# Moving half of a convolution's multiplier out of the attention loop and into a seven-product step

## The chip, the cores and the metric

The kernel runs on one core of one Trainium2 chip. The metric is device time in microseconds (us). Before the change it is 686.75 us, the median of 3 runs (686.73 to 687.19).

## The reference, cut to what matters

One layer on x with 512 positions and 1024 channels. After a norm, one projection `h @ w_in` gives the multiplier B, C and the input of a gated convolution (512 channels each), q, k and v of 8 heads, and the gates. Cut:

```python
cb, cc, cin, q, k, v, f_logit, g_logit = jnp.split(proj, split_idx, axis=-1)
u = causal_dwconv(cc * cin, conv_mix_w[l])
y_conv = (cb * u) @ w_out_conv[l]
...
o = forgetting_attention(q, k, v, log_f)
y_attn = o @ w_out_attn[l]
x = x + (g_conv * y_conv + g_attn * y_attn) @ w_o[l]
```

The multiplier of the convolution, `cb`, is what the change computes in another way. A feed-forward part and a last norm follow.

## The kernel before

**Numbers.** All products are in fp32r. Each fp32 operand is kept as a high and a low part, and a product is three matmuls (high by high, low by high, high by low). A weight block arrives by DMA as a tile `raw`; ScalarE (ACT) makes the high part `wh` (L275), VectorE (DVE) the low part `wl` (L282), in two buffers each, so that block n+2 can be split only when TensorE (PE) is done with block n. A matmul of these steps has 256 columns.

**Plain and seven-product steps.** A plain output block of 128 channels by 512 positions takes 8 input blocks, 3 matmuls, 2 halves: 48 matmuls (`proj`). `seven` computes a pair of output blocks over pairs of input blocks and halves of the positions with 7 products where 8 would do (a Strassen-Winograd form): 84 matmuls for the pair and not 96. It needs sums of input blocks (`xt`, split into `xtq` by `x_split`), and sums of weights: a chunk `P` holds three weight blocks as they are for each step, a chunk `F` four sums of weight blocks, which DMAs add up in DRAM ahead (`make_forms`: a copy on SP's queue, then an accumulating DMA on POOL's queue, three times over, six transfers for a form). A pair is two steps, so four chunks: P, F, P, F, with 18, 24, 18 and 24 matmuls. Its results come out of four PSUM banks by DVE and ACT work (`z1`, `m1`, `u3`, `m2`, then one `fin` for each block).

**Order of the work.** Projections for v, q0, k0, q1, k1 come first. Then the attention loop: 37 rounds, one for each unit (pair of heads, head, block of 128 queries) and five more to finish. A round has the scores of one unit (`s`), a part of the remaining projections as filling (`p_in`; a list `late` of 16 blocks: C, input and B of the convolution and q, k of heads 4 to 7), the transposes of the unit of three rounds ago (`tp`, with ACT and DVE parts `pth`, `ptl`), and, when four units are complete, the product with v (`o`, in `attend`). The result `o` is taken out of PSUM in two halves, each by an ACT copy (L727, one head) and then a DVE add (L728), four instructions in a chain, ACT, DVE, ACT, DVE; then it is split again into `oth` and `otl`. Lists `behind` and `later` hold evacuation work until a later place in the code. The convolution's `taps` are an ACT scale (L616) and two DVE instructions (L617, L620) on a product that POOL makes (L637).

**Banks.** In the loop `p_in` and `o` take turns in PSUM banks 0, 1, 7 (`acc`), with 16 blocks and 8 `o`: 24 turns, so that the last `o` has bank 7. `s` has banks 2, 3, 4 and `tp` 5, 6.

**After the loop.** For j = 0 to 7, `seven` makes the pair of gates j (banks 3, 4, 0, 1), then `yc` and `ya` multiply the convolution's and attention's results by block `mix j` (24 matmuls each). `yc` reads the convolution's four blocks `ych`, `ycl` in order. Projections with `wo`, the feed-forward part (`p_up`, `dn`) and the last norm follow.

**Queues.** SP's queue carries the weight loads and the copies of the sums, POOL's queue the adding transfers, beside POOL's own arithmetic. `slot()` starts those transfers whose turn it is: once a round in the loop, three times for each gate pair.

An engine runs its instructions in the order in which they are listed, and the builder sets that order engine by engine.

Of the kernel before, what the change touches and what calls it, by code (L numbers as in the profile page):

```python
# [63 lines left out]
UPD = tuple(tuple(((j, q), (j, q + 1)) for j in js for q in (0, 2)) for js in SUP)  # L64
DOUBLES = GATES + UPD[0] + STEPS[0] + UPD[1] + STEPS[1]
NU = [len(GATES), len(GATES + UPD[0] + STEPS[0])]
ND = [NU[i] + len(UPD[i]) for i in range(2)]
GROUPS = {"gate": (2, 4, 3), "up0": (2, 4, 1), "up1": (2, 4, 1), 0: (2, (0, 3, 14, 18, 22, 26), 1), 1: (2, 3, 1)}


@with_exitstack
def block_kernel(ctx, tc, xT, vecs, xv, win, wmix, wo, wup, wst, wdp, outT):
# [10 lines left out]
    def keep(ins):  # L83
        return tc.keep_in_program_order(ins)
# [101 lines left out]
    def make_forms(n0, n1, key, start=0):  # L186
# [7 lines left out]
        for g, (a, b) in enumerate(zip(cuts, cuts[1:])):  # L194
# [438 lines left out]
    def evac_cin(i):  # L633
        def f(p):
            z, u = ct(f"z{i}"), ct(f"u{i}")
            nc.vector.tensor_mul(z, p, rb1)
            nc.gpsimd.tensor_mul(z, z, cst[i])  # L637
            cst[i] = u
            behind.append(lambda: taps(u, z, CM + 3 * i))

        return f

    def evac_cb(i):
        def f(p):
            y = ct(f"y{i}")
            nc.vector.tensor_mul(y, p, rb1)
            if i < 3:
                nc.gpsimd.tensor_mul(y, y, cst[i])

            def split_y():  # L650
                if i == 3:
                    nc.vector.tensor_mul(y, y, cst[i])
                nc.scalar.activation(ych[:, i, :], y, AF.Copy)
                nc.vector.tensor_sub(ycl[:, i, :], y, ych.bitcast(F32)[:, i, :])

            if i < 3:
                behind.append(split_y)
            else:
                later.append((k_mix - 1, 1.4, (("yc", i),), split_y))

        return f


# [319 lines left out]

    make_forms(NU[0], ND[0], "up0")
    for j in range(KB):
        for _ in range(3):
# [3 lines left out]
        gs = []  # L990
        seven(GATES[2 * j : 2 * j + 2], 2 * j, {j: GSETS}, gate_form, done=gate_pair(j, gs))
# [487 lines left out]
def _layout(i):  # L1479
# [97 lines left out]
```

## Time and profile before

| | |
|---|---|
| median of 3 runs | 686.75 us (686.73 to 687.19) |
| the profiled execution | 687.1 us |
| its span, first to last instruction | 685.3 us |
| granted clock, mean | 0.998 |
| PE busy | 678.4 us (99%) |
| DVE, ACT, POOL busy | 565.9, 373.7, 194.8 us |
| attention loop | 52.5 to 171.0 us |
| eight gate pairs with yc and ya | 171.0 to 290.9 us |

A matmul's row in the timeline gives its start and its modelled length; matmuls overlap, so the pace is read from starts. "A <- B" in a row means that A's engine sat idle and B's end released it. PEld is the load of weights into the array.

### The profile page before, as it was taken

What the parts mean: (1) busy time and instruction counts of PE and PEld (TensorE: products, weight loads), DVE (VectorE), ACT (ScalarE), POOL (GpSimd) and SP (SyncE); (2) the same over time, 40 slices, a digit from 0 to 9 for tenths busy, and PEclk for the clock granted to TensorE, in tenths of its full rate; (3) what the DMA queues carried; (4) which work ended last, traced back from release to release, by engine and by line L of the source; (5) the groups of instructions that cost most, each with busy time, mean ns of one, the idle gap of its engine ahead of it and who ended that gap; (6) DMA issues with size and microseconds to landing.
All of it is one profiled execution on the core that took longest, in us unless ns stands there. A gap on an engine that the chain in (4) does not pass through costs nothing.

```text
span 685.3 us, 14704 instructions
## 1 busy us (share of the span) xinstructions
PE 678.4 (99%) x5902; PEld 677.0 (99%) x5902; DVE 565.9 (83%) x884; ACT 373.7 (55%) x594; POOL 194.8 (28%) x204
## 2 busy tenths in 40 slices
PE   9999999999999999999999999999999999999996
PEld 9999999999999999999999999999999999999996
DVE  6898778787787778769879699998787799998894
ACT  7775566566454444546664554546445555445673
POOL 0537775541030201114500144340100314332000
PEclk9999999999999999999999999999999999999999
DMA  9469999744498596868997498888945986776513
GB/s 331 145 159 261 295 216 273 153 96 130 157 252 240 160 333 201 250 227 211 159 319 241 122 247 212 191 230 257 260 140 192 290 253 164 172 190 158 199 33 123
DMA packets 68197, 141.21 MB, mean 206 GB/s; under 512 B 6016, under 2 KB 32128, under 8 KB 67872
## 3 DMA queue, kind: packets, MB, share of 16 engines
q1 hardware_dynamic: 46760, 110.85, 48.1%
q0 software_dynamic: 19920, 26.01, 24.9%
q10 hardware_dynamic: 1448, 3.42, 1.3%
q8 instruction: 46, 0.75, 0.4%
q14 instruction: 23, 0.19, 0.1%
HBM read 135.99 MB, written 51.90 MB: 274 GB/s over the span
## 4 chain that ended last, share of the span: by engine, by line
PE 98%; issue 1%; DVE 0%; POOLq 0%
PE dn L331 32%; PE p_up L313 21%; PE p_in L313 13%; PE p_up L331 6%; PE p_wo L313 6%; PE ya L313 3%; PE yc L313 3%; PE pa L525 2%; PE pb L527 2%; PE p_q L313 2%; PE p_k L313 2%; PE o L719 2%; PE tp L702 1%; PE pdA L313 1%; PE s L672 1%; PE s L673 1%
## 5 line engine op out<-in xcount | busy, mean ns | idle before, releaser
L313 PE MATMUL p_up<-x1hl,wh_up 128*128 128x256 f32 x832 | 133.7, 276 | 0.0
L313 PEld LDWEIGHTS p_up<-x1hl,wh_up 128*128 128x128 f32 x832 | 112.3, 188 | 0.0
L208 POOL DMA_DIRECT2D f<-in_wst_dram x75 | 79.8, 1244 | 32.7 <-DMA f<-f 30.1
L313 PE MATMUL p_up<-x1hl,wl_up 128*128 128x256 f32 x416 | 81.1, 276 | 0.0
L282 DVE TENSOR_TENSOR wl_F<-raw_F,wh_F 128x1024 fp32r<-128x1024 f32 (+1 forms) x47 | 61.4, 1306 | 21.4 <-ACT wh_F L275 21.2
L275 ACT ACTIVATE wh_F<-raw_F 128x1024 fp32r<-128x1024 f32 (+1 forms) x47 | 48.7, 1037 | 44.2 <-PE dn L331 26.7
L313 PEld LDWEIGHTS p_up<-x1hl,wl_up 128*128 128x128 f32 x416 | 62.7, 188 | 0.0
L275 ACT ACTIVATE wh_P<-raw_P 128x768 fp32r<-128x768 f32 (+1 forms) x47 | 38.7, 822 | 35.9 <-PE dn L331 24.8
L1246 POOL TENSOR_TENSOR ge<-fu,fu 128x512 f32<-128x512 f32 x11 | 21.7, 1969 | 125.1 <-DVE fu L620 93.6
L282 DVE TENSOR_TENSOR wl_P<-raw_P,wh_P 128x768 fp32r<-128x768 f32 (+1 forms) x47 | 45.1, 961 | 14.3 <-ACT wh_P L275 7.3
L331 PE MATMUL dn<-gh,wh_F 128*128 128x256 f32 x216 | 51.0, 276 | 0.0
L331 PE MATMUL dn<-gl,wh_F 128*128 128x256 f32 x216 | 51.0, 276 | 0.0
L313 PE MATMUL p_in<-xgh,wh_in 128*128 128x256 f32 x256 | 50.6, 279 | 0.0
L313 PE MATMUL p_in<-xgh,wl_in 128*128 128x256 f32 x256 | 50.4, 278 | 0.0
L282 DVE TENSOR_TENSOR wl_up<-raw_up,wh_up 128x1024 fp32r<-128x1024 f32 x34 | 45.1, 1326 | 6.2 <-ACT wh_up L275 6.1
L313 PE MATMUL p_in<-xgl,wh_in 128*128 128x256 f32 x256 | 50.2, 277 | 0.0
L275 ACT ACTIVATE wh_up<-raw_up 128x1024 fp32r<-128x1024 f32 x34 | 35.8, 1054 | 22.4 <-PE p_up L313 11.6
L1003 POOL TENSOR_TENSOR xt<-xt 128x512 f32<-128x512 f32 x8 | 11.0, 1376 | 104.6 <-DVE xt L1002 104.6
L313 PEld LDWEIGHTS p_in<-xgh,wh_in 128*128 128x128 f32 x256 | 39.9, 188 | 0.7
L331 PEld LDWEIGHTS dn<-gh,wh_F 128*128 128x128 f32 x216 | 40.6, 188 | 0.0
L331 PEld LDWEIGHTS dn<-gl,wh_F 128*128 128x128 f32 x216 | 40.5, 188 | 0.0
L616 ACT ACTIVATE fu<-fz,vec 128x512 f32<-128x512 f32 x34 | 24.4, 719 | 28.9 <-DVE fz L1182 27.7
(320 smaller groups left out, 2087.5 us busy)
## 6 DMA issues: line engine op xcount, KB each, us to landing
raw_F<-f SPq DMA_DIRECT2D x44, 512.0 KB, 5.3
raw_up<-in_wup_dram SPq DMA_DIRECT2D x34, 512.0 KB, 4.5
raw_P<-in_wst_dram SPq DMA_DIRECT2D x44, 384.0 KB, 5.5
f<-in_wst_dram POOLq DMA_DIRECT2D x45, 256.0 KB, 8.3
f<-in_wst_dram SPq DMA_DIRECT2D x21, 512.0 KB, 6.6
f<-in_wst_dram POOLq DMA_DIRECT2D x21, 512.0 KB, 10.0
f<-f SPq DMA_DIRECT2D x42, 256.0 KB, 6.7
raw_in<-in_win_dram SPq DMA_DIRECT2D x20, 512.0 KB, 7.3
```

What stands on the lines that cost most here:

```text
L208: make_forms.add = keep(nc.gpsimd.dma_start(dst, src, accum_op=ALU.add)).ins
L275: ins = nc.scalar.activation(hi, raw, AF.Copy)
L282: ins = nc.vector.tensor_sub(lo[:, cs], r, hi.bitcast(F32)[:, cs])
L313: keep(nc.tensor.matmul(out[:, cs], w, x[:, cs], start=start and i == 0 and c == 0, stop=stop and i == 2 and c == len(cut) - 1,))
L331: keep(nc.tensor.matmul(out, wl if x == 1 else wh, xl if x == 2 else xh, start=opens and bk not in seen, stop=closes and bk not in left,))
L525: keep(nc.tensor.matmul(pa[t][:, :VW], xk, w[:, VB:], start=start, stop=stop))
L527: keep(nc.tensor.matmul(pb[t], xk, w[:, :VB], start=start and t % 2 == 0, stop=stop and t % 2 == 1))
L616: nc.scalar.activation(u, z, AF.Copy, scale=col(w + 2))
L672: keep(nc.tensor.matmul(s[:, :nn], QT[pr][:, e, qs], KA[pr][:, e, :nn], start=True, stop=False))
L719: keep(nc.tensor.matmul(o[:, 2 * P * e + c0 : 2 * P * (e + 1)], w, x[:, kb, c0:], start=e == 0 and kb == 0 and i == 0, stop=e == 1 and kb ...
L1003: nc.gpsimd.tensor_add(a, a, b)
L1246: keep(nc.gpsimd.tensor_mul(ge, a.rearrange(halves_of, h=2), b.rearrange(halves_of, h=2)))
```

## The change

Four edits. **The pair:** blocks 2 and 3 of the multiplier (`CB = (1,)`, one pair) leave the list `late`, and `seven` computes them as the pair `CONV` between the loop and the first gate pair, in banks 3, 4, 0, 1; the gate pairs now have banks 7, 5, 2, 6, and `yc`, `ya` take turns in 0, 1, 3, 4. Their `fin` multiplies by a tile `cst`, which POOL made as u times the norm's rows (`u_rows`), and then splits. **The transfers:** a form's six transfers are five rounds apart (four before), and nine forms start at rounds 0, 2, 5, 9, 13, 17, 21, 25, 29; some of them now end among the gate pairs. **The outputs:** the split of blocks 0 and 1 comes one round later than before. **The head:** x and v blocks 2 and 3 are loaded in two DMAs each, and the vector of constants in two.

```diff
+CB = (1,)
+CONV = tuple(((c, q), (c, q + 1)) for c in CB for q in (0, 2))
...
-GROUPS = {"gate": (2, 4, 3), "up0": (2, 4, 1), "up1": (2, 4, 1), 0: (2, (0, 3, 14, 18, 22, 26), 1), 1: (2, 3, 1)}
+GROUPS = {"gate": (2, 5, (0, 2, 5, 9, 13, 17, 21, 25, 29)), "up0": (2, 4, 1), "up1": (2, 4, 1), 0: (2, (0, 3, 14, 18, 22, 26), 1), 1: (2, 3, 1)}
...
-    conv_i = [[4 + i, 8 + i, i] for i in range(4)]
+    conv_i = [[4 + i, 8 + i, i][: 2 if i // 2 in CB else 3] for i in range(4)]
...
-    xcuts = sorted(xcuts + [xcuts[kb + 2] + S for kb in (4, 5, 6, 7)])
+    xcuts = sorted(xcuts + [xcuts[kb + 2] + S for kb in (2, 3, 4, 5, 6, 7)])
...
-    keep(nc.sync.dma_start(vec, vecs))
+    for cs in (slice(0, CF), slice(CF, NV)):
+        keep(nc.sync.dma_start(vec[:, cs], vecs[:, cs]))
...
             cst[i] = u
-            behind.append(lambda: taps(u, z, CM + 3 * i))
+
+            def u_rows():
+                cst[i] = xt[:, CB.index(i // 2) * 2 + i % 2, :]
+                nc.gpsimd.tensor_mul(cst[i], u, rb1)
+
+            def tap():
+                taps(u, z, CM + 3 * i)
+                if i // 2 in CB:
+                    behind.append(u_rows)
+
+            behind.append(tap)
...
+            behind.append(lambda: behind.append(lambda: split_y(i, y)))
...
             def fin(n):
+                def y():
+                    nc.vector.scalar_tensor_tensor(
+                        gs[n], gs[n], (1.0, -1.0)[n], cst[2 * j + n], op0=ALU.mult, op1=ALU.mult
+                    )
+                    split_y(2 * j + n, gs[n])
...
-    GSETS = (3, 4, 0, 1)
+    GSETS = (7, 5, 2, 6)
+    CSETS = ((3, 4, 0, 1),)
...
-    assert not fill and not todo_bg and not behind
+    while behind:
+        with after_split():
+            behind.pop(0)()
+    assert not fill
...
-    acc = ring(2, 5, 6, 7)
+    acc = ring(0, 1, 3, 4)
...
+    for n, c in enumerate(CB):
+        seven(CONV[2 * n : 2 * n + 2], 2 * n, {c: CSETS[n]}, gate_form, done=gate_pair(c, [], True))
     for j in range(KB):
...
+        if j == 0:
+            flush([("y", c) for c in CB])
         yc, ya = acc(f"yc{j}"), acc(f"ya{j}")
```

How this moves instructions is seen at three places. In the names, `p_in3` is the fourth block of B, `p_in11` the fourth block of the convolution's input, `o31` the last `o`, `oc31` its copy out of PSUM, `dnABC` a result of `seven` in bank C, `z3` and `u3` the last product and taps of the convolution. "Waits" names the engine whose count the instruction waits for.

**PE, the end of the attention loop.** Before:

```order
L313 MATMUL p_in3_2382<-xgl_95,wh_in3_2285 128x256 x2
L719 MATMUL o31_2461<-pth301_2304,v2_116 128x256 [waits DVE_49,Activation_49]
L719 MATMUL o31_2461<-ptl311_2337,v2_116 128x256 [waits DVE_49]
L719 MATMUL o31_2461<-ptl311_2337,v2_116 128x256 x2
L719 MATMUL o31_2461<-ptl311_2337,v2_116 128x128
L331 MATMUL dn000_2508<-xgh_94,wh_P0_2374 128x256
```

And now:

```order
L319 MATMUL p_in11_2270<-xgl_95,wh_in11_2153 128x256 x2
L729 MATMUL o31_2352<-pth301_2200,v2_116 128x256 [waits DVE_49,Activation_49]
L729 MATMUL o31_2352<-ptl311_2231,v2_116 128x256 [waits DVE_49]
L729 MATMUL o31_2352<-ptl311_2231,v2_116 128x256 x2
L729 MATMUL o31_2352<-ptl311_2231,v2_116 128x128
L337 MATMUL dn010_2397<-xgh_94,wh_P0_2264 128x256 [waits DVE_49,PE_49]
```

The loop's three banks now have 22 turns, and the last `o` falls on bank 0, which is also the bank of the first product of the new pair. That matmul had no wait before; it now waits until DVE's second add has taken `o31` out of the bank.

**DVE, the same place.** Before:

```order
L620 SCALAR_TENSOR_TENSOR u3_2379<-z3_2378,vec_64,u3_2379 128x510 [waits DVE_49]
L282 TENSOR_TENSOR wl_F0_2454<-raw_F0_2153,wh_F0_2453 128x1024 [waits DMAHW0_49,Activation_49]
L646 TENSOR_TENSOR y3_2457<-p_in3_2382,rb_n1_545 128x512 [waits PE_49]
L882 TENSOR_TENSOR xtq_448<-xt_103,xtq_448 128x1024 [waits DMASW3_49,DMASW1_49,Activation_49]
L728 TENSOR_TENSOR oc31_2478<-o31_2461,oc31_2478 64x256 [waits Activation_49]
L282 TENSOR_TENSOR wl_P1_2557<-raw_P1_2283,wh_P1_2556 128x768 [waits DMAHW1_49,PE_49,Activation_49]
L728 TENSOR_TENSOR oc31_2478<-o31_2461,oc31_2478 64x256 [waits Activation_49]
```

And now:

```order
L288 TENSOR_TENSOR wl_F0_2340<-raw_F0_2019,wh_F0_2339 128x1024 [waits DMAHW1_49,Activation_49]
L643 TENSOR_TENSOR z3_2343<-p_in11_2270,rb_n1_550 128x512 [waits PE_49]
L892 TENSOR_TENSOR xtq_452<-xt_103,xtq_452 128x1024 [waits DMASW7_49,DMASW0_49,Activation_49]
L738 TENSOR_TENSOR oc31_2369<-o31_2352,oc31_2369 64x256 [waits Activation_49]
L624 SCALAR_TENSOR_TENSOR u3_2344<-z3_2343,vec_64,u3_2344 128x511 [waits Activation_49]
L738 TENSOR_TENSOR oc31_2369<-o31_2352,oc31_2369 64x256 [waits Activation_49]
```

The convolution's last block of input is now the last filling, so its taps stand between the two adds that empty `o31`; before, they were done ahead of both. ACT has the same order: copy, the taps' scale (which waits for POOL's product), copy.

**ACT and DVE, the end of the first gate pair, ahead of `yc0`.** ACT now:

```order
L281 ACTIVATE wh_F3_2594<-raw_F3_2495 128x1024 [waits DMAHW1_49,DVE_49,PE_49]
L281 ACTIVATE wh_mix0_2624<-raw_mix0_2531 128x1024 [waits DMAHW6_49,DVE_49,PE_49]
L281 ACTIVATE wh_P4_2686<-raw_P4_2563 128x768 [waits DMAHW7_49,DVE_49,PE_49]
L670 ACTIVATE ych_98<-xt_103 128x512 [waits DVE_49] x2
L912 ACTIVATE xt_103<-dn202_2511 128x256 [waits PE_49]
```

DVE now:

```order
L288 TENSOR_TENSOR wl_mix0_2625<-raw_mix0_2531,wh_mix0_2624 128x1024 [waits DMAHW6_49,PE_49,Activation_49]
L933 SCALAR_TENSOR_TENSOR xt_103<-xt_103 128x512
L933 SCALAR_TENSOR_TENSOR xt_103<-xt_103 128x512 [waits DVE_49,Pool_49]
L288 TENSOR_TENSOR wl_P4_2687<-raw_P4_2563,wh_P4_2686 128x768 [waits DMAHW7_49,PE_49,Activation_49]
L671 TENSOR_TENSOR ycl_99<-xt_103,ych_98 128x512 [waits Activation_49] x2
L913 TENSOR_TENSOR xt_103<-dn202_2511,xt_103 128x256 [waits Activation_49]
```

On DVE before, ahead of the first `yc`:

```order
L282 TENSOR_TENSOR wl_mix0_2613<-raw_mix0_2451,wh_mix0_2612 128x1024 [waits DMAHW3_49,PE_49,Activation_49]
L652 TENSOR_TENSOR y3_2457<-y3_2457,u3_2379 128x512
L654 TENSOR_TENSOR ycl_99<-y3_2457,ych_98 128x512 [waits Activation_49]
L903 TENSOR_TENSOR xt_103<-dn000_2508,xt_103 128x256 [waits Activation_49]
L907 TENSOR_TENSOR xt_103<-dn003_2506,xt_103 128x512 [waits DVE_49]
```

Blocks 2 and 3 of `ych` and `ycl` now both come after the split of the next gate pair's first chunk, P4, on ACT and on DVE, and P4's split waits for PE's last matmul of the first gate pair (its buffers are those of the chunk F3). Before, only block 3 was still open there, and it was split ahead of that chunk. The third and fourth block of `yc0` wait for these.

More of the change, by code (lines that the diff above doesn't have):

```diff
@@ L64 @@
 UPD = tuple(tuple(((j, q), (j, q + 1)) for j in js for q in (0, 2)) for js in SUP)
-DOUBLES = GATES + UPD[0] + STEPS[0] + UPD[1] + STEPS[1]
-NU = [len(GATES), len(GATES + UPD[0] + STEPS[0])]
+DOUBLES = CONV + GATES + UPD[0] + STEPS[0] + UPD[1] + STEPS[1]
+NU = [len(CONV + GATES), len(CONV + GATES + UPD[0] + STEPS[0])]
 ND = [NU[i] + len(UPD[i]) for i in range(2)]
-GROUPS = {"gate": (2, 4, 3), "up0": (2, 4, 1), "up1": (2, 4, 1), 0: (2, (0, 3, 14, 18, 22, 26), 1), 1: (2, 3, 1)}
+GROUPS = {"gate": (2, 5, (0, 2, 5, 9, 13, 17, 21, 25, 29)), "up0": (2, 4, 1), "up1": (2, 4, 1), 0: (2, (0, 3, 14, 18, 22, 26), 1), 1: (2, 3, 1)}
 @with_exitstack
@@ L133, in step_chunks @@
         return [(f"P{n}", wst[n, :, : 3 * m * P], 3 * m * P), (f"F{n}", n, 4 * m * P)]
+    for n in range(len(CONV)):
+        stream += step_chunks(n)
+    n = len(CONV)
     for j in range(KB):
@@ L213, in make_forms @@
             ops = (put(f0, x0), add(f0, x1), put(f1, f[:, :, :m]), add(f1, x1[:, :, m:]), put(f2, f1), add(f2, x2))
-            todo_bg.extend((start + (step * k if isinstance(step, int) else step[k]) + shift * g, op) for k, op in enumerate(ops))
+            at = start + (shift * g if isinstance(shift, int) else shift[g])
+            todo_bg.extend((at + (step * k if isinstance(step, int) else step[k]), op) for k, op in enumerate(ops))
         todo_bg.sort(key=lambda w: w[0])
@@ L492, in block_kernel @@
     scales = ((), (), (0, 1), (2,), (3,), (4, 5), (6,), (7,))
-    make_forms(0, len(GATES), "gate")
+    make_forms(0, NU[0], "gate")
     for kb in range(KB):
@@ L646, in f, with split_y @@
             nc.vector.tensor_mul(y, p, rb1)
[L647 to L659, printed above, removed]
-        return f
+            nc.gpsimd.tensor_mul(y, y, cst[i])
+            behind.append(lambda: behind.append(lambda: split_y(i, y)))
+        return f
+    def split_y(i, y):
+        nc.scalar.activation(ych[:, i, :], y, AF.Copy)
+        nc.vector.tensor_sub(ycl[:, i, :], y, ych.bitcast(F32)[:, i, :])
     PT, PA = {}, {}
@@ L874, in mt @@
         return xt[:, (mt.n - 1) % KB, :]
-    mt.n = 0
+    mt.n = 2 * len(CB)
     def x_split(q):
@@ L891, in gate_form, with gate_pair @@
         return xqh[:, QPOS[q], i], xql[:, QPOS[q], i]
-    def gate_pair(j, gs):
+    def gate_pair(j, gs, conv=False):
         def done(i, banks, ids):
@@ L925, in f @@
                     nc.scalar.activation(g, g, AF.Sigmoid, bias=col(BG + 8 * n + j), scale=(1.0, -1.0)[n])
-                return f
-            for f, us, x in ((z1, 0.42, 2), (m1, 0.7, 0), (u3, 0.85, 3), (m2, 0.7, 1), (fin(0), 0.7, None), (fin(1), 0.7, None)):
-                later.append((0, us, () if x is None else (ids[x],), f))
-        return done
-    GSETS = (3, 4, 0, 1)
+                return y if conv else f
+            for f, us, x in ((z1, 0.42, 2), (m1, 0.7, 0), (u3, 0.85, 3), (m2, 0.7, 1), (fin(0), 1.4 if conv else 0.7, None), (fin(1), 1.4 if conv else 0.7, None)):
+                later.append((0, us, (("y", j),) if x is None else (ids[x],), f))
+        return done
+    GSETS = (7, 5, 2, 6)
+    CSETS = ((3, 4, 0, 1),)
     fill = []
@@ L990, in block_kernel @@
         gs = []
-        seven(GATES[2 * j : 2 * j + 2], 2 * j, {j: GSETS}, gate_form, done=gate_pair(j, gs))
+        seven(GATES[2 * j : 2 * j + 2], len(CONV) + 2 * j, {j: GSETS}, gate_form, done=gate_pair(j, gs))
         wh, wl = chunk(f"mix{j}")
+        if j == 0:
+            flush([("y", c) for c in CB])
         yc, ya = acc(f"yc{j}"), acc(f"ya{j}")
@@ L1527, in _layout @@
     wdn = blocks(i["w_down"][0]).reshape(KB, P, NP, P)
+    wcb = win[:4].reshape(4, P, KB, P)
     wga = blocks(wi[:, o + H :]).reshape(2, KB, P, KB, P).transpose(1, 0, 2, 3, 4).reshape(2 * KB, P, KB, P)
@@ L1530, in _layout @@
     wu4 = wup.reshape(2 * NP, P, KB, P)
-    for w4, d in [(wga, d) for d in GATES] + [(wu4, d) for d in UPD[0]] + [(wdn, d) for d in STEPS[0]] + [(wu4, d) for d in UPD[1]] + [(wdn, d) for d in STEPS[1]]:
+    for w4, d in [(wcb, d) for d in CONV] + [(wga, d) for d in GATES] + [(wu4, d) for d in UPD[0]] + [(wdn, d) for d in STEPS[0]] + [(wu4, d) for d in UPD[1]] + [(wdn, d) for d in STEPS[1]]:
         def pick(*which):
```

1 line of the change is left out of this document (removed).

## The prediction

> **What bounds the kernel now.** I read the page's busy times first, then PE's waits, then the chain that ended last, then the timeline where the change acts. The page, and PE's waits in full (in total, times, longest):
>
> ```profile
> PE 678.4 (99%) x5902; PEld 677.0 (99%) x5902; DVE 565.9 (83%) x884; ACT 373.7 (55%) x594; POOL 194.8 (28%) x204
> ```
>
> ```profile
> PE pc_n L348 <- ACT sq L1414: 0.9, 1, 0.9
> PE warm L117 <- PEq L1563: 0.8, 1, 0.8
> ```
>
> PE waits twice, at the very start and in the last norm, and never in the attention loop or behind it. So each matmul that goes is worth its full pace, and each wait that a change adds costs its full length. From the chain (start, length, what):
>
> ```profile
> 164.08 2.77 PE p_in L313 x24
> ...
> 171.14 9.60 PE dn L331 x84
> 180.74 2.72 PE yc L313 x24
> ```
>
> A filling matmul of the loop takes 2.77 / 24 = 0.115 us, one of `yc` 2.72 / 24 = 0.113, a seven-product pair 9.60 for 84. The loop as a whole, as a window (length; busy us of PE, PEld, DVE, ACT, POOL; granted clock; DMA):
>
> ```profile
> 52.50:171.00 118.50, 118.50 (x1009) 117.79 (x1007) 94.15 (x210) 71.33 (x159) 68.34 (x82) 1.00 0.84 202
> ```
>
> **The pair: what goes.** Two plain blocks are 96 matmuls of 0.115 = 11.1 us; the pair costs 9.6. PE's own work falls by 1.5 us (1.36 if all twelve matmuls fewer go at 0.113). That is the whole gain, and about what a measurement of this kernel can tell from no change (0.2% of 686.75 is 1.4 us).
>
> **The pair: what it waits for.** The last `o` now lies in bank 0, and the pair's first matmul writes bank 0. So PE stands still until DVE's second add has emptied the bank, and behind that matmul stands all of PE's queue. How long emptying takes where nothing is in the way, from the `o` of four rounds earlier:
>
> ```profile
> 161.10 0.39 PE L719 MATMUL o<-ptl,v 128*128 128x256 f32 x2
> ...
> 161.53 0.38 ACT L727 ACTIVATE oc<-o 64x256 f32<-64x256 f32 x1 [0.37 <-PE o L719]
> ...
> 161.94 0.42 DVE L728 TENSOR_TENSOR oc<-o,oc 64x256 f32<-64x256 f32 x1 [0.20 <-ACT oc L727]
> ...
> 162.39 0.38 ACT L727 ACTIVATE oc<-o 64x256 f32<-64x256 f32 x1 [0.48 <-DVE oc L728]
> ...
> 162.80 0.43 DVE L728 TENSOR_TENSOR oc<-o,oc 64x256 f32<-64x256 f32 x1 [0.44 <-ACT oc L727]
> ```
>
> From 161.49 to 163.23 is 1.8 us with PE's restart: the lower end. At the end of the loop more is in the way:
>
> ```profile
> 169.18 0.56 PE L719 MATMUL o<-pth,v 128*128 128x256 f32 x4
> 169.38 1.06 ACT L275 ACTIVATE wh_F<-raw_F 128x1024 fp32r<-128x1024 f32 x1 [0.88 <-PE p_in L313]
> ...
> 170.35 1.05 ACT L881 ACTIVATE xtq<-xt 128x1024 fp32r<-128x1024 f32 x1
> 170.47 1.23 DVE L282 TENSOR_TENSOR wl_F<-raw_F,wh_F 128x1024 fp32r<-128x1024 f32 x1 [0.21 <-ACT wh_F L275]
> ...
> 170.98 0.33 PE L331 MATMUL dn<-xgh,wh_P 128*128 128x256 f32 x1
> ...
> 171.62 0.68 DVE L646 TENSOR_TENSOR y<-p_in,rb_n 128x512 f32<-128x512 f32 x1
> ...
> 172.22 1.22 DVE L882 TENSOR_TENSOR xtq<-xt,xtq 128x1024 fp32r<-128x1024 f32 x1
> ...
> 173.35 0.41 DVE L728 TENSOR_TENSOR oc<-o,oc 64x256 f32<-64x256 f32 x1
> ...
> 173.79 0.38 ACT L727 ACTIVATE oc<-o 64x256 f32<-64x256 f32 x1 [0.33 <-DVE oc L728]
> ...
> 174.66 0.43 DVE L728 TENSOR_TENSOR oc<-o,oc 64x256 f32<-64x256 f32 x1
> ```
>
> The filling ends at 169.18; PE goes on at 170.98 though bank 7 is not empty until 175.09, since nobody wants bank 7. The changed order, on these times: DVE has the low part of F until 171.70, then the last filling's evacuation, now the convolution's `z` in the place of `y`, until 172.30, then `xtq` until 173.44 and the first add until 173.76. Then come the taps of that `z`, and DVE may not go to the second add before them. What they need is seen where they ran before:
>
> ```profile
> 165.20 0.69 DVE L636 TENSOR_TENSOR z<-p_in,rb_n 128x512 f32<-128x512 f32 x1
> ...
> 165.97 1.28 POOL L637 TENSOR_TENSOR z<-z,cc 128x512 f32<-128x512 f32 x1 [6.44 <-DVE z L636]
> ...
> 166.40 1.94 DVE L882 TENSOR_TENSOR xtq<-xt,xtq 128x1024 fp32r<-128x1024 f32 x1
> ...
> 167.29 0.73 ACT L616 ACTIVATE u<-z,vec 128x512 f32<-128x512 f32 x1 [1.71 <-POOL z L637]
> ...
> 168.26 0.74 DVE L617 SCALAR_TENSOR_TENSOR u<-z,vec,u 128x511 f32<-128x511 f32 x1
> ```
>
> POOL starts 0.08 behind `z`: 172.38, and ends 1.28 later at 173.66. ACT's scale runs 173.70 to 174.43, its second copy of `o` behind it to 174.81. DVE's tap runs 174.47 to 175.21, the second add to 175.64. PE goes on at about 175.7 where it went on at 170.98: **a wait of 4.7 us**. Beside POOL's product `xtq` can take 1.94 and not 1.22, which moves the first add to 174.16 and the last only by 0.1. The ends are 1.8 (taps out of the way) and 5.5 (each step 0.2 slower); I take 4.7, since every step has its row.
>
> **What the wait does to the clock.** The start and the end of the run:
>
> ```profile
> 0.77 3.76 PE warm L117 x16
> ```
>
> ```profile
> 4.82 0.64 PE L525 MATMUL pa<-wl_v,xgh 128*128 128x264 f32 x2
> ...
> 6.70 0.41 PE L525 MATMUL pa<-wl_v,xgh 128*128 128x264 f32 x2
> ```
>
> ```profile
> 678.70:682.10 3.40, 1.36 (x12) 1.00 0.28 104
> 682.10:685.30 3.20, 0.00 (x0) 0.51 0.58 220
> ```
>
> In the last window PE is done with its 12 matmuls after 1.36 us, at 680.06; about 2.1 us later the granted clock is 0.51. At the start PE works from 0.77; two matmuls span 0.64 us at 4.8 and 0.41 at 6.7, so the full pace comes some 5.5 us after the first work. So a pause of 4.7 us is over twice what sufficed at the end, and I expect the clock to fall in it or just behind it. The price: at half pace for t us PE loses t / 2. The upper end is the start's 5.5 us, 2.7 us lost; the lower is zero. The loss can begin late in the pause, so I take some 4 us at half pace, 2.0 us lost, nearer to the start's row.
>
> **The third and fourth block of the first `yc`.** Their splits stand on ACT and DVE behind the split of chunk P4. The rows for the pieces:
>
> ```profile
> 177.42 1.06 ACT L275 ACTIVATE wh_mix<-raw_mix 128x1024 fp32r<-128x1024 f32 x1 [0.94 <-ACT wh_F L275]
> 178.52 1.22 DVE L282 TENSOR_TENSOR wl_mix<-raw_mix,wh_mix 128x1024 fp32r<-128x1024 f32 x1 [0.78 <-ACT wh_mix L275]
> ...
> 180.38 0.63 ACT L653 ACTIVATE ych<-y 128x512 fp32r<-128x512 f32 x1 [1.89 <-DVE y L652]
> ...
> 181.04 0.69 DVE L654 TENSOR_TENSOR ycl<-y,ych 128x512 fp32r<-128x512 f32 x1 [0.70 <-ACT ych L653]
> 181.18 0.84 ACT L275 ACTIVATE wh_P<-raw_P 128x768 fp32r<-128x768 f32 x1
> ...
> 182.83 0.95 DVE L282 TENSOR_TENSOR wl_P<-raw_P,wh_P 128x768 fp32r<-128x768 f32 x1
> ```
>
> Let 0 be the end of the first gate pair on PE, where `yc0` starts. The chunk before the last ends 24 matmuls earlier, at -2.7; then mix0's high part takes ACT until -1.5 and its low part DVE until -0.25; the two products for blocks 2 and 3 (0.68 each, as `y` above) take DVE until 1.1. P4's high part starts when PE is done, 0.15 to 1.0; then ACT makes `ych` 2 until 1.65 and 3 until 2.3. DVE makes P4's low part until 2.05, `ycl` 2 until 2.75, 3 until 3.45. PE wants `ych` 2 at 12 x 0.113 = 1.36 and gets it at 1.7; four matmuls later, at 2.15, it wants `ycl` 2 and gets it at 2.8; the rest follows by 3.7 where it would have been 2.72. **A second wait of 1.0 us**, in two pieces. Its ends: zero, if the products come earlier, and 2.3, if all of DVE's lateness (3.45 against 1.1) is handed on to the next gate pair.
>
> **Edits that I cost at nothing.** Shorter rounds: the loop loses 11.1 of 118.5 us of filling, while ACT, DVE and POOL keep nearly all their work; DVE goes from 94 of 118.5 us to at most 94 of 107.4, 88%, and PE has no wait in the loop to lengthen. Without that cover the loop would keep its length (a rival). The head's finer loads: PE works without a wait from 4.2 us on, so nothing is gained or lost but perhaps 0.2 us either way. The transfers:
>
> ```profile
> f<-in_wst_dram POOLq DMA_DIRECT2D x45, 256.0 KB, 8.3
> ```
>
> An adding transfer takes 8.3 us; five rounds of 107.4 / 37 = 2.9 us are 14.5. So what POOL's queue waits for has landed, and `z`'s product behind such a transfer isn't held up. The later splits of blocks 0 and 1 are read tens of us later.
>
> **The sum.** On the profiled execution, 687.1: -1.5 + 4.7 + 2.0 + 1.0 = +6.2, so 693.3. That execution lies 0.35 above the median of the runs, so on the median 692.95, say 693.0.
>
> **The rivals.** *The clock holds* through the pause: 691.0. For it: at the end of the run PE's work had been thin for some us before the clock fell, here it is dense on both sides. The Trainium skill, "TensorE: Matmul & The Clock Gate", Part 1, says that the clock halves after a whole idle window of about 3.4 us, and that windows run free of the program. By that, as an estimate, a pause of 4.7 us holds a whole window in (4.7 - 3.4) / 3.4, some 4 of 10 cases, and the time would be 691.0 in the other 6; the row at the end of the run, a fall after 2.1 us of rest, goes further than this rule, and I weigh the row more.
>
> *The bank is free sooner*, not slower: if POOL's product and the taps' scale are done by the time of the first add, the second follows it at once and the wait is the 1.8 us of the earlier `o`; then the clock holds, and with the second wait also gone the sum is -1.5 + 1.8 = +0.3, 687.05. It decides where the wait falls under 2.9 us. Against it: `z` can't start before 171.6, and its four steps have rows.
>
> *No wait shows at all* and the twelve matmuls are the whole result: 685.25. Against it: the adds read what the last `o` writes, so the bank can't be free at once.
>
> *The loop keeps its length*, bound by DVE or POOL: the pair's 9.6 comes on top and nothing goes, 696.4. Against it: PE's empty list of waits.
>
> **How the numbers follow.** Clock falls 0.54, clock holds 0.29, bank free sooner 0.08, no wait 0.04, loop keeps its length 0.05. The predicted time is the first. Its own range is 691.4 to 695.0 (clock loss 1.0 to 2.7, second wait 0.4 to 2.3). The range reaches down to 689.6, the second rival with the wait at 4.3 and no wait at `yc0`, and up to 695.0. Faster by over 0.2%: 0.04. Within: 0.08. Slower: the rest, 0.88.
>
> **What would show it.** Right: PE's waits list the pair's first matmul behind DVE's L738, 4 to 5 us; the timeline has the tap between the two adds of `oc`; matmuls of the pair start 0.21 apart for some us; a wait of 0.3 to 0.7 twice in the first `yc`; the loop is shorter by about 11 us. Wrong: no wait of PE ahead of the pair, or one under 2.9; a pair at the full pace at once (then the clock held); new waits of PE inside the loop.

## The result and the profile after

The changed kernel takes 703.54 us (median of 4 runs, 701.83 to 705.3) beside 686.74 for the kernel before on the same chip: a ratio of 1.0243 (95% interval 1.0213 to 1.0273). It is slower, as forecast, but by 17 us and not by 6: the range on record ended at 695.0. The profiled execution takes 702.5 us, its span is 700.7.

The busy times of the changed kernel, from its page; each is close to that of before, and PE's share has fallen from 99 to 97%:

```profile
span 700.7 us, 14726 instructions
PE 682.3 (97%) x5890; PEld 678.5 (97%) x5890; DVE 570.3 (81%) x890; ACT 375.5 (54%) x597; POOL 198.7 (28%) x208
```

PE's waits in the changed kernel (in total, times, longest). The two of before are still there (left out); these are new:

```profile
PE dn L337 <- DVE oc L738: 5.4, 1, 5.4
PE tp L712 <- DVE ptl L716: 1.3, 1, 1.3
PE o L729 <- DVE cc L636: 1.1, 1, 1.1
...
PE yc L319 <- DVE wl_mix L288: 0.8, 1, 0.8
PE tp L712 <- POOL pp L696: 0.7, 2, 0.4
PE yc L319 <- ACT wh_mix L281: 0.5, 1, 0.5
PE o L729 <- DVE ptl L716: 0.5, 1, 0.5
PE yc L319 <- ACT ych L670: 0.4, 1, 0.4
PE yc L319 <- DVE ycl L671: 0.3, 1, 0.3
PE tp L712 <- POOL xtq L612: 0.2, 1, 0.2
```

They fall into three places. The first is the wait for bank 0 (`dn` behind `oc`, 5.4). The second is the loop, which had no wait of PE before (`tp` and `o`: 1.3 + 1.1 + 0.7 + 0.5 + 0.2 = 3.8). The third is the first `yc` (0.8 + 0.5 + 0.4 + 0.3 = 2.0).

The stages, measured from the starts of PE's instructions in the timelines (us). `s` is the first score, so that the second row is the loop:

| stage | before | after | difference | predicted |
|---|---|---|---|---|
| start to first `s` | 52.26 | 51.58 | -0.68 | 0 |
| first `s` to last `o` | 118.66 | 112.86 | -5.80 | -11.1 |
| last `o` to first `dn` | 0.06 | 5.62 | +5.56 | +4.7 |
| first `dn` to first `yc` | 9.59 | 22.48 | +12.89 | +9.6 + 2.0 |
| first `yc` to last `ya` | 110.05 | 113.20 | +3.15 | +1.0 |
| from there to PE's last | 389.17 | 389.46 | +0.29 | 0 |
| sum | | | +15.4 | +6.2 |

The difference of the spans is 700.7 - 685.3 = 15.4, so nothing lies outside these rows. In the loop 5.3 us of the forecast gain are missing, and its listed waits are 3.8 of them; the other 1.5 stand in no wait of the list.

The wait for bank 0, as a chain of the changed kernel (start, length, what):

```profile
163.84 1.22 DVE wl_F L288
165.06 0.61 DVE z L643
...
165.74 2.18 POOL z L644
...
167.94 0.73 ACT u L623
...
168.70 0.75 DVE u L624
...
169.48 0.44 DVE oc L738
...
170.06 11.56 PE dn L337 x76
```

These are the steps that the prediction lists, in its order: the low part of F, `z`, POOL's product, ACT's scale, DVE's tap, the second add, PE. Only POOL's product has another length than I took, 2.18 for 1.28. And the chain's 11.56 us for 76 matmuls of the pair, 0.152 each and not 0.114, shows the clock. As windows of the changed kernel (length; PE, PEld, DVE, ACT, POOL busy; granted clock; DMA):

```profile
165.19:168.61 3.42, 0.00 (x0) 0.00 (x0) 1.93 (x3) 0.67 (x1) 2.17 (x1) 1.00 0.50 164
168.61:175.44 6.83, 5.38 (x25) 5.42 (x26) 3.22 (x5) 1.69 (x4) 2.32 (x2) 0.50 0.19 20
```

The clock is at half from 168.61 to 175.44. PE works in it from 170.06, 5.38 us, and so loses 2.7.

### The profile page after: what moved, and what is told of

It is laid out like the page before. It is cut to its first block, busy times and chain, and to the rows that moved or that the text cites. A ratio compares the mean times of both kernels' runs of the same rounds, so it can differ in the third digit from the quotient of the medians.

```text
span 700.7 us, 14726 instructions
## 1 busy us (share of the span) xinstructions
PE 682.3 (97%) x5890; PEld 678.5 (97%) x5890; DVE 570.3 (81%) x890; ACT 375.5 (54%) x597; POOL 198.7 (28%) x208
## 3 DMA queue, kind: packets, MB, share of 16 engines
q10 hardware_dynamic: 1448, 3.42, 1.3%
## 4 chain that ended last, share of the span: by engine, by line
PE 70%; DVE 13%; ACT 7%; issue 4%; DMA 4%; POOL 2%; POOLq 0%; ACTq 0%; DVEq 0%
PE dn L337 31%; PE p_up L319 20%; PE p_up L337 6%; PE ya L319 3%; PE yc L319 3%; DVE wl_in L288 2%; PE pa L532 2%; PE pb L534 2%; DMA raw_P<-in_wst_dram 1%; DVE xtq L613 1%; DMA f<-f 1%; ACT wh_in L281 1%; PE p_wo L319 1%; DMA f<-in_wst_dram 1%; DVE s L687 1%
## 5 line engine op out<-in xcount | busy, mean ns | idle before, releaser
L213 POOL DMA_DIRECT2D f<-in_wst_dram x78 | 84.7, 1294 | 29.3 <-DMA f<-f 28.5
L288 DVE TENSOR_TENSOR wl_F<-raw_F,wh_F 128x1024 fp32r<-128x1024 f32 (+1 forms) x49 | 64.3, 1313 | 23.6 <-ACT wh_F L281 23.5
L281 ACT ACTIVATE wh_F<-raw_F 128x1024 fp32r<-128x1024 f32 (+1 forms) x49 | 50.8, 1037 | 45.6 <-PE dn L337 32.2
L281 ACT ACTIVATE wh_P<-raw_P 128x768 fp32r<-128x768 f32 (+1 forms) x49 | 40.3, 823 | 41.1 <-PE dn L337 27.6
L288 DVE TENSOR_TENSOR wl_P<-raw_P,wh_P 128x768 fp32r<-128x768 f32 (+1 forms) x49 | 47.3, 966 | 18.2 <-ACT wh_P L281 10.9
L319 PE MATMUL p_in<-xgh,wh_in 128*128 128x256 f32 x224 | 44.4, 279 | 0.0
L319 PE MATMUL p_in<-xgh,wl_in 128*128 128x256 f32 x224 | 44.1, 278 | 0.0
L319 PE MATMUL p_in<-xgl,wh_in 128*128 128x256 f32 x224 | 43.9, 278 | 0.0
L319 PEld LDWEIGHTS p_in<-xgh,wh_in 128*128 128x128 f32 x224 | 35.1, 189 | 0.7
```

Of the source, the lines that this page charges most:

```text
L213: make_forms.add = keep(nc.gpsimd.dma_start(dst, src, accum_op=ALU.add)).ins
L281: ins = nc.scalar.activation(hi, raw, AF.Copy)
L288: ins = nc.vector.tensor_sub(lo[:, cs], r, hi.bitcast(F32)[:, cs])
L319: keep(nc.tensor.matmul(out[:, cs], w, x[:, cs], start=start and i == 0 and c == 0, stop=stop and i == 2 and c == len(cut) - 1,))
```

## The experiments

The experiments are called e1 to e11, in the order of their sections. Two questions were open. Where do the loop's 5.3 us come from? And are the four places (loop, bank, clock, first `yc`) separate prices, or does one wait only take the place of another? My theory after the traces: the loop is bound by DVE and the waits that ACT imposes on it, so that PE's filling was a cover; the waits at `yc` come from loads that are issued late. Its rival: DVE's evacuations and splits are late behind the loop anyway, so that whatever is removed comes back one step later.

### The last `o` in bank 7

```diff
-    acc, bank_s, bank_t = ring(0, 1, 7), ring(2, 3, 4), ring(5, 6)
+    acc, bank_s, bank_t = ring(7, 0, 1), ring(2, 3, 4), ring(5, 6)
```

> The changed kernel with the loop's banks taken in the order 7, 0, 1, so that the last o has bank 7 and the pair's first matmul finds bank 0 free. If the wait for the bank and the clock that falls in it are a cost of their own (5.5 us of standing, 5.45 us at half pace, 2.7 us lost), the time falls by about 8, to 695 to 696, PE's waits hold no dn ahead of the pair, and the granted clock stays at 1.00. Rival: DVE is late anyhow, and PE waits at the pair's next chunks for their splits; then it falls by half of that or less, to 699 or more.

Measured: 699.18 us (698.9 to 699.57), ratio to before 1.0182 (1.0166 to 1.0197). PE's waits behind the loop in this kernel:

```profile
PE yc L319 <- ACT wh_mix L281: 4.1, 1, 4.1
...
PE yc L319 <- DVE wl_mix L288: 0.5, 1, 0.5
```

The wait for the bank is gone: the last `o` starts at 164.46, the pair's first matmul at 164.52. But only 4.4 us come back, and the clock still falls, at 187.9, again for 6.83 us. The rival was right that the wait moves on. What it waits for now is seen in the chain:

```profile
177.16 10.23 DMA raw_mix<-in_wmix_dram
...
187.50 1.06 ACT wh_mix L281
...
188.58 1.24 DVE wl_mix L288
```

It is a load, and not DVE's splits.

### A loop with its old length of filling

```diff
             for kb in range(KB * i // n, KB * (i + 1) // n):
                 ...
+            if i == 0 and n == KB:
+                mm3(st["p"], wh[:, :P], wl[:, :P], xgh[:, 0, :], xgl[:, 0, :], True, True)
```

> The changed kernel with 84 matmuls more in the loop: the first input block of each of the 14 filling blocks is multiplied twice, with the same result. DVE, ACT and POOL have the same work. If the loop's waits (some 4.9 us ahead of tp and o) come from PE being faster than the chain through DVE and ACT, they go: 9.7 us of matmuls are added, and the time rises by 5 only, to 708 to 709. Rival: they come from the transfers or the later splits; then it rises by all of 9.7, to 713.

Measured: 709.03 us (708.94 to 709.33), ratio 1.0324 (1.0307 to 1.0341). All of PE's waits in the loop are gone; the list of this kernel holds only the bank, the first `yc`, and the two of before (left out):

```profile
PE dn L337 <- DVE oc L740: 5.6, 1, 5.6
PE yc L319 <- ACT wh_mix L281: 3.0, 1, 3.0
...
PE yc L319 <- DVE wl_mix L288: 0.8, 1, 0.8
```

84 matmuls more are worth 84 x 0.115 = 9.7 us of PE, and the time rose by 5.5. The loop by itself, from the first `s` to the last `o`, rose by 4.6, from 112.86 to 117.45, so that 5.1 us of the matmuls took the place of time that PE had lost there. Between the two profiled executions the rest of the rise lies mostly behind the loop, where the first `yc` waits for 3.8 us and the clock falls a second time, at 200.69 for 3.41 us.

### The kernel before with less filling

```diff
+                if n == KB and kb == KB - 1:
+                    continue
-                mm3(st["p"], wh[:, ks], wl[:, ks], xgh[:, kb, :], xgl[:, kb, :], kb == 0, kb == KB - 1)
+                mm3(st["p"], wh[:, ks], wl[:, ks], xgh[:, kb, :], xgl[:, kb, :], kb == 0, kb == KB - 1 - (n == KB))
```

> The kernel before with the last of the eight input blocks left out of each of the 16 filling blocks of the loop: 96 matmuls less there, and nothing else of the change. If DVE and ACT have no room to go faster in the loop, PE now waits in it for tp and o, and of the 11.1 us only 5 to 7 are gained: 680 to 682. Rival, as in the prediction: the loop shrinks by all of it, 675.7, with no new waits of PE.

Measured: 682.73 us (682.0 to 683.88), ratio 0.9943 (0.9928 to 0.9958). This is the step of my prediction by itself, on the kernel before: this kernel leaves out the last input block of each filling block, so that 11.1 us of filling go and no instruction of DVE, ACT or POOL does. The time falls by 3.8, a little less than I expected, and the loop by 4.6, from 118.66 to 114.06. The longest waits of PE that appear in its loop:

```profile
PE tp L704 <- DVE ptl L708: 1.8, 3, 0.6
PE tp L704 <- DVE m L687: 1.1, 2, 0.7
...
PE o L721 <- DVE ptl L708: 0.5, 1, 0.5
```

### The three other edits without the pair

On the kernel before: the transfers (here 2, 5, 3), the head's loads of x and v, the constants in two loads, and the splits of all outputs of the convolution a round later.

```diff
-GROUPS = {"gate": (2, 4, 3), ...
+GROUPS = {"gate": (2, 5, 3), ...
...
-    xcuts = sorted(xcuts + [xcuts[kb + 2] + S for kb in (4, 5, 6, 7)])
+    xcuts = sorted(xcuts + [xcuts[kb + 2] + S for kb in (2, 3, 4, 5, 6, 7)])
...
-                behind.append(split_y)
+                behind.append(lambda: behind.append(split_y))
```

> The kernel before with the change's three other edits and without the pair: loads of the head cut finer, transfers of the sums five rounds apart (starts still three apart), the convolution's splits one round later. If these cost nothing, 686.2 to 687.5. Rival: the loop's waits are theirs; then 690 to 692, with PE waiting in the loop for tp or o.

Measured: 687.0 us (686.54 to 688.18, 10 runs), ratio 1.0006 (0.9997 to 1.0015). No wait of PE is added. By themselves these edits cost nothing, as predicted; the loss comes with the pair. (The nine uneven starts of the changed kernel's transfers were not tried without it.)

### The transfers of the next stage one gate pair later

What stands ahead of `raw_mix` on SP's queue, in the changed kernel (start, length, issue):

```profile
180.09 1.92 SPq L208 DMA_DIRECT2D f<-in_wst_dram  x3
182.11 0.77 SPq L183 DMA_DIRECT2D raw_mix<-in_wmix_dram  x1
183.99 0.33 SPq L183 DMA_DIRECT2D raw_P<-in_wst_dram  x1
```

And in the kernel before:

```profile
164.86 0.33 SPq L178 DMA_DIRECT2D raw_mix<-in_wmix_dram  x1
165.24 1.92 SPq L203 DMA_DIRECT2D f<-in_wst_dram  x3
```

There the load of the first `mix` goes ahead of the three copies for the feed-forward sums; now the copies go first, because the pair's four chunks stand ahead of `mix` in the stream and the copies are still started where the first gate pair begins. The edit moves those copies behind the load, and sets the six steps of a form three slots apart and not four:

```diff
-..., "up0": (2, 4, 1), ...
+..., "up0": (2, 3, (3, 6, 6)), ...
```

> The changed kernel, with the transfers for the first feed-forward sums begun one gate pair later, so that the loads of the first mix block and of the next two chunks go ahead of three 512-KB copies on SP's queue. Late-load theory (the 2.6 us of waits in the first yc come from those copies, behind which the chunk P4 took 10.11 us to land): P4 lands 3 us or more earlier, the first yc waits at most the 1.0 us that I predicted from the splits alone, and the time is 703.5 - 1.6 to 2.6 = 701 to 702. The wait for bank 0 (5.5) and the clock's fall behind it (6.83 us at half pace) stay. Rival (the splits' order on ACT and DVE sets those waits, not the load): the waits stay at 2.6 and the time at 703.5.

Measured: 698.7 us (698.5 to 698.99), ratio 1.0173 (1.0158 to 1.0188). The gain is 4.8, more than the theory gave; between the two profiled executions it is 3.5. The loads of `raw_mix` in this stretch land within 6.0 us, where those of the changed kernel and of e1 took 10.2; all waits of the first `yc` are gone from PE's list. Stage by stage the profiles differ by 1.7 us from the first `dn` to the first `yc`, and by 2.35 from there to the last `ya`. Of the 1.7, 0.9 is the clock: here it falls earlier in the same pause (167.26), so that PE works 3.5 us at half pace and not 5.4. The 3.42 us ahead of that fall, as a window:

```profile
163.84:167.26 3.42, 0.87 (x7) 0.57 (x5) 3.42 (x5) 1.28 (x2) 1.02 (x1) 1.00 0.54 139
```

The late loads were thus worth some 3 us, in front of `yc` as well as in it.

### Both

The last `o` in bank 7 and the later transfers.

> Both at once: the last o in bank 7 as in e1_bank, and the later transfers as in e5_puts. Late-load theory: the 4.1 us wait of yc for the high part of mix0, which e1_bank showed, goes with the 10.23 us of its load; the clock then has no pause to fall in and stays at 1.00 up to the end; left over are the loop's waits (some 4.9 us) and up to 1 us in yc. 686.6 - 1.5 + 4.9 + 0 to 1.0 = 690 to 691. Rival (what is behind the loop is bound by DVE's evacuations and splits, so that the wait moves on once more): 696 to 699, with a wait of 3 us or more elsewhere and the clock down behind it.

Measured: 693.38 us (693.21 to 693.87), ratio 1.0096 (1.0081 to 1.0111). The clock doesn't fall before the end of the run. The longest waits are those of the loop, and one of 0.7 in the first `yc`:

```profile
PE tp L712 <- DVE ptl L716: 1.3, 1, 1.3
...
PE yc L319 <- DVE ycl L671: 0.7, 1, 0.7
```

So the bank, the loads and the clock are removable, together 10.2 us. That is still 2 to 3 us over what I expected. From the first `dn` to the last `ya` this kernel takes 132.1 us, where 119.6 and the pair's 9.5 (84 of 0.1134) would make 129.2: 2.9 us over, with the listed 0.7 among them. The rest lies in pauses of 0.1 to 0.3 at the seams of the chunks between 164 and 200, where the kernel before has one of 0.05. At two of the seams PE waits for DVE's low part of F, which takes 2.07 us at 171.63 and 2.19 at 193.47, each time beside a product on POOL, where the two low parts of F between them take 1.21 and 1.22 without one. No run tried the seams by themselves.

### Work for PE during the wait

```diff
+    wm = bank_t("warm2")
+    for _ in range(44):
+        keep(nc.tensor.matmul(wm[:, : 2 * P], xgh[:, 0, :P], xgh[:, 1, : 2 * P], start=True, stop=True))
     acc = ring(0, 1, 3, 4)
```

> The changed kernel, with 44 matmuls of 256 columns more (44 x 0.113 = 5.0 us) into an idle bank between the last o and the pair, that nobody reads: PE works through nearly all of the 5.5 us for which it waits for bank 0. Nothing is freed sooner, so only the clock can change. Clock theory (the 6.83 us at half pace are a price of their own, 2.7 us lost): the granted clock stays at 1.00 there and the time is 703.5 - 2.7 = 700.8. Rival (the half pace costs nothing, since DVE or a load is late next): the time stays at 703.5, with 2 to 3 us of new waits in the first yc.

Measured: 700.98 us (699.81 to 701.58), ratio 1.0204 (1.0188 to 1.0219). The pair's first matmul starts at 169.93 as before, PE no longer idles ahead of it, and the clock holds through the pair: from the first `dn` to the first `yc` 20.18 us instead of 22.48. The clock's fall was thus a price of its own: 2.3 us in this stage, and 2.6 of the median, where its row gave 2.7. The 2.6 is a net figure, since the clock falls later in this kernel too, for 3.41 us, as a window shows:

```profile
188.44:191.85 3.41, 1.84 (x14) 1.43 (x13) 1.76 (x3) 1.90 (x2) 0.00 (x0) 1.00 0.94 284
```

Ahead of the fall at 191.85 PE was busy for 1.84 of 3.41 us, with two waits of the first `yc`, of 0.8 us each, within it.

### Less work for DVE in the loop

On the kernel with both repairs, every second filling block makes no low part; its matmuls read the low part of the block before it.

```diff
-            for x in "hl":
+            spare = k in [n for n, c in enumerate(stream) if c[0][:2] == "in"][-14:][1::2]
+            for x in "h" if spare else "hl":
...
-        hi, lo = hl
+        hi, lo = hl if len(hl) == 2 else (hl[0], parts[k - 1][1])
...
-        cuts = ...
+        cuts = [] if len(hl) == 1 else ...
```

> e6_both, but every second one of the 14 filling blocks makes no low part: its matmuls read that of the block before it (the output isn't the reference's). DVE has 7 x 1.23 = 8.6 us less to do in the loop; PE has as many matmuls, ACT and POOL as much work. Cover theory (the loop's waits come from DVE's work and its waits for ACT, in a loop that is too short for them): PE's waits in the loop fall from some 4.9 us to under 1, the loop comes to some 107.5 us, and the time is 686.6 - 1.5 + 0 to 1.0 = 685 to 686.5, under before. Rival (ACT or POOL bounds the loop): the loop's waits stay, 690 to 691 like e6_both.

Measured: 688.71 us (688.18 to 690.09, 7 runs), ratio 1.0029 (1.0017 to 1.004). The loop's waits fall to 0.3, and the loop, from first `s` to last `o`, to 108.3 us. So the cover theory holds for the loop: with less work on DVE alone, and that of ACT and POOL unchanged, PE's waits go. The loop as a window in three kernels (each window begins 0.3 to 1.1 us behind the first `s`); first the one with both repairs, then this one, then the kernel before with less filling (e3):

```profile
52.30:164.60 112.30, 108.91 (x913) 107.08 (x911) 88.31 (x203) 68.06 (x155) 67.29 (x82) 1.00 0.93 207
```

```profile
52.30:159.60 107.30, 107.00 (x906) 106.13 (x905) 79.57 (x194) 68.40 (x155) 65.14 (x81) 1.00 0.95 215
```

```profile
52.70:166.40 113.70, 109.64 (x911) 107.15 (x910) 93.38 (x209) 71.27 (x160) 67.67 (x81) 1.00 0.86 211
```

Length less DVE's busy time is 24.0, 27.7 and 20.3 us: DVE idles for 20 us and more even where PE waits for it. The time of the whole kernel missed my 685 to 686.5 by over 2 us, by the same pauses at the seams as in the kernel with both repairs (132.3 us from the first `dn` to the last `ya`).

### The low parts on POOL

To have DVE's relief with the whole computation, POOL makes the low part of every second filling block.

```diff
-            ins = nc.vector.tensor_sub(lo[:, cs], r, hi.bitcast(F32)[:, cs])
+            spare = k in [n for n, c in enumerate(stream) if c[0][:2] == "in"][-14:][1::2]
+            sub = nc.gpsimd.tensor_sub if spare else nc.vector.tensor_sub
+            ins = sub(lo[:, cs], r, hi.bitcast(F32)[:, cs])
```

> e6_both, with the low part of every second of the 14 filling blocks made by POOL and no longer by DVE: the whole computation, and DVE has as little in the loop as in e8_low. POOL's price isn't in the traces; its product of 128x512 takes 1.28 to 2.18 us, so 128x1024 some 2.6 to 4.4, seven of them 18 to 31 us on top of POOL's 67. Cover theory, with POOL in time: the loop comes to some 107.5 to 108.5 us and the time to that of e8_low, 688 to 690. Rival (POOL's part comes late, or slows DVE beside it): PE waits in the loop for a POOL low part, 693 or more.

Measured: 697.96 us (697.63 to 698.87), ratio 1.0162 (1.0147 to 1.0177): worse than without it. The group of the seven low parts on POOL in this kernel's loop (busy, mean ns; idle before), and the longest of PE's waits:

```profile
L290 POOL TENSOR_TENSOR wl_in<-raw_in,wh_in 128x1024 fp32r<-128x1024 f32 x7 | 17.7, 2532 | 3.3 <-ACT wh_in L281 2.5 <-POOL xtq L614 0.7
```

```profile
PE tp L714 <- DVE ptl L718: 5.8, 4, 3.1
PE s L685 <- DMA xtq<-fr: 1.1, 1, 1.1
```

No wait of PE is for a POOL low part. PE waits for DVE's `ptl` more than before, and for a transfer that POOL's queue issues (`xtq<-fr`). What stands ahead of the longest wait is seen in the timeline of this kernel:

```profile
85.68 2.38 POOL L290 TENSOR_TENSOR wl_in<-raw_in,wh_in 128x1024 fp32r<-128x1024 f32 x1 [1.68 <-ACT wh_in L281]
...
86.53 3.09 DVE L615 TENSOR_TENSOR xtq<-t_q,xtq 64x512 fp32r<-64x512 f32 x2 [0.30 <-ACT xtq L613]
...
89.65 0.69 DVE L718 TENSOR_TENSOR ptl<-tp,pth 128x512 fp32r<-128x512 f32 x1
...
90.49 0.30 PE L714 MATMUL tp<-ident,pp 128*128 128x128 f32 x1 [3.06 <-DVE ptl L718]
```

DVE's two `xtq` take 3.09 us beside POOL's low part, where the kernel with both repairs has 1.70 for the two (at 85.97), and `ptl`, for which PE waits, stands behind them. By these rows POOL's low part slowed DVE, which is the second half of the rival. For the other waits, that POOL's work comes later behind the low parts is only argued. The clock fell too, at 91.96, behind this wait.

### `ya` ahead of `yc`

On the kernel just shown, in the first gate pair only.

```diff
-        for pp, hh, ll, o in ((yc, ych, ycl, 0), (ya, oth, otl, 4)):
+        both = ((yc, ych, ycl, 0), (ya, oth, otl, 4))
+        for pp, hh, ll, o in both[::-1] if j == 0 else both:
```

> e9_pool, and in the first gate pair ya (whose operands have long been ready) goes ahead of yc, which gives the splits of blocks 2 and 3 another 24 x 0.113 = 2.7 us. Theory of the splits (the 0.7 us for which yc waits for a low part in e6_both is the part that I predicted as the second wait): that wait goes, 0.7 to 0.8 us under e9_pool. Rival (the splits are late for another reason, or the next gate pair takes the wait over): as e9_pool.

Measured: 697.98 us (697.59 to 698.35), ratio 1.0161 (1.0144 to 1.0178): the same as without it. The wait for `ycl` is gone, and in its place stands

```profile
PE dn L339 <- ACT wh_F L281: 1.3, 2, 1.0
```

The next pair's sums took the wait over. Here the rival holds: the time is the same whether PE meets the late splits in `yc` or in the next pair.

### The low parts on POOL in the kernel before

The same edit, over 16 filling blocks.

> The kernel before, with the low part of every second of its 16 filling blocks made by POOL. PE has no waits in its loop, so by the cover theory there is nothing to gain: 686.6 to 687.0, the same as before. Rival (low parts on POOL shorten or lengthen the loop by themselves, so that e9_pool says nothing of the pair): away from 686.8 by over 1.5 us.

Measured: 695.02 us (694.17 to 695.29), ratio 1.0115 (1.01 to 1.013). My theory gave no change; that was wrong. The loop as a window of this kernel:

```profile
52.40:179.00 126.60, 120.82 (x1011) 118.44 (x1010) 91.83 (x202) 71.10 (x159) 85.20 (x91) 1.00 0.80 189
```

POOL is busy for 85 of 126.6 us, DVE for less time than before, and the loop is 8 us longer. So "DVE's busy time sets the loop" is too simple: a round is a chain through DVE, ACT and POOL, and an engine at two thirds of its time can lengthen it. Two ways are seen in this trace. Beside POOL's low part of 83.85 to 86.72 DVE's two `xtq` take 4.32 us, and the kernel before has 1.70 for them. And DVE's waits for the taps' scale on ACT, which itself waits for POOL's product, grow from the 3.2 us of before to 9.1. What each is worth was not tried. By this result the runs with low parts on POOL say nothing for or against the pair.

## Why the prediction was wrong, point by point

- **The sign and the mechanism of the largest term: right.** The pair's first matmul waits for DVE's second add, with the taps of the last `z` between the two adds, step by step as worked out. The bank in which the last `o` lies is the cause: with bank 7 the wait is gone (e1).
- **The wait for bank 0, 4.7: mis-sized, 5.56.** POOL's product took 2.18 and not 1.28, beside DVE's `xtq`, which had started just ahead of it. I had let `xtq` stretch beside POOL's product but not the other way round.
- **The clock, 2.0: right in kind, mis-sized, 2.7.** It is a separate price: work in the pause takes it away (e7). The half pace lasted 6.83 us, with PE at work for 5.38 of them, and not the 4 that I took. The rival in which it holds was wrong in the profiled execution. But the row that I weighed, a fall after 2.1 us of rest, was among the shortest: e8's kernel rests for 5.1 us at its end with the clock still full.

```profile
681.70:686.80 5.10, 0.00 (x0) 0.00 (x0) 1.48 (x3) 0.37 (x1) 1.27 (x1) 1.00 0.55 206
```

  A pause of 4.7 us thus need not have brought a fall, and how much of the half pace PE meets depends on where the fall lies in the pause: 2.7 us were lost here and 1.8 in e5. The Trainium skill, "TensorE: Matmul & The Clock Gate", Part 1, has the clock halve after one whole idle window of 3.4 us; ahead of this fall such a window lies, 165.19 to 168.61 with no work of PE, which agrees.
- **The first `yc`, 1.0: mis-sized, and for another reason.** Where loads and bank are out of the way, `yc` waits 0.7 for `ycl` (e6), which is the term that I worked out. But the stages around it lost some 3 us more to loads behind three copies on SP's queue (e5). I had read POOL's queue for the transfers and not where SP's loads now stand: the order of that queue was in front of me, and `mix` behind the copies could have been seen there.
- **"Shorter rounds", costed at nothing: the step that failed.** The text said that DVE would go "from 94 of 118.5 us to at most 94 of 107.4, 88%, and PE has no wait in the loop to lengthen". The loop fell by 5.8 and not by 11.1, so that 5.3 us of the 9.2 by which the sum fell short are this step's. On the kernel before alone, 11.1 us less filling bring 3.8, and 4.6 in the loop (e3); with the filling back the waits are gone (e2); with less for DVE to do they fall to 0.3 us (e8). The rival "the loop keeps its length" had the mechanism, at a chance of 0.05, with half its price; its 696.4 left out the waits for the bank and what the clock costs.

What the 88% left out is a view that I didn't read: DVE's own waits in the loop of before. Their longest, in the kernel before (in total, times, longest):

```profile
DVE m L685 <- ACT pp L681: 5.2, 9, 0.9
DVE wl_in L282 <- ACT wh_in L275: 4.1, 7, 1.1
DVE u L617 <- ACT u L616: 3.2, 2, 1.7
DVE ptl L706 <- ACT pth L705: 2.9, 4, 1.1
...
DVE s L677 <- PE s L673: 0.6, 1, 0.6
```

DVE was idle for 24 of the 118.5 us, but hardly any of it was spare time behind PE: PE ended 0.6 us of it, ACT nearly all the rest (some 22). I counted the 24 us as room, and most of it wasn't. In e3, where DVE keeps its work (93.7 us), they shrank to 20.3 while the loop went to 114.06, and PE already waited for 4 us there. In the changed kernel DVE's own work in the loop fell as well, from 94.3 to 88.9 us, and its idle time stayed at 24.0: the loop lost little more than DVE's work did, 5.8 against 5.4, and DVE's share is 79% as before, not the 88% of my text. How short the chain's waits can get was not tried beyond e3.

- **Transfers, head, later splits at nothing: right by themselves** (e4, 1.0006).
- **The pair's saving of 1.5 us** was never seen as a gain. No kernel with the pair beat the kernel before: with both repairs it is at 1.0096, and with seven low parts left out as well at 1.0029.

## What to carry to other kernels

An engine's busy share doesn't say how far a loop can shrink: read who ends its idle time, and count what other engines of the same chain end as part of the loop's length. When work is moved, follow every queue past the place where it stood, the loads' as well as the arithmetic's, and count the turns of the PSUM ring to see which bank the last user holds. Work that is moved to another engine can slow the engine that it was taken from. A short pause of TensorE can cost its length and then the half pace behind it, and filling the pause with idle matmuls shows the two apart.

## What the runs showed of the hardware that was not expected

- **The clock falls without a whole idle stretch.** All falls inside the runs lasted 3.41 or 6.83 us, one or two stretches of 3.41 us. Eight of them were seen, and only three (the changed kernel, e1 but for 0.03 us, the first of e2) have 3.41 us without work of PE just ahead. Ahead of the others PE was busy for 0.3 us of the 3.41 (e10), 0.5 (the second of e2), 0.9 (e5, window above), 1.5 (e9) and 1.84 (e7, the kernel with work in the pause, window above). By the Trainium skill's rule ("TensorE: Matmul & The Clock Gate", Part 1, a whole idle window) it would have held in that kernel, wherever the windows lie, since no wait of PE in it is longer than 1.3 us; the measurement goes further than the rule. The busy share alone doesn't decide it either: in e8 PE was busy for 1.63 of the 3.41 us up to 683.43, less than in e7, and the clock held. What decides it stays open.
- **POOL and DVE beside each other stretch one of the two.** In the kernel before, POOL's product started first (165.97, 1.28 us) and DVE's `xtq` took 1.94. In the changed one `xtq` started first, and took 1.22, and the product (165.74, in the chain above) 2.18:

```profile
165.58 1.22 DVE L892 TENSOR_TENSOR xtq<-xt,xtq 128x1024 fp32r<-128x1024 f32 x1
```

  In these two cases the later one paid, and so it did where the two met elsewhere: with `xtq` first the product took 2.20 in e1, e8 and e9, and with a product first `xtq` took 2.01 (before, 150.10) and 1.95 (the changed kernel, 135.69). In e9 two `xtq` took 3.09 and not 1.70 behind a low part on POOL. No run tried it by itself. The Trainium skill, "GPSIMD Engine Reference", section 1, says that POOL shares its SBUF interfaces with DVE, with contention where a DVE instruction has two SBUF inputs, as `xtq` has; the rows agree.
- **A low part of 128x1024 takes POOL 2.53 us** (mean of seven in e9), where DVE takes 1.23.
